# Max-pool and subtract: the first tile loaded in pieces of 1, 1 and 2 rows

## The chip, the cores and the metric

One core of one Trainium2 chip runs the program. The metric is the device time of one execution in microseconds (us). The profile's span is 1.7 to 1.8 us shorter than that time, because it begins with the first and ends with the last recorded instruction. VectorE is called DVE in the profile, the queue that issues loads SP, the queue that issues stores ACT. "Packet" means one of the transfers that a DMA engine makes; the trace records each one with its start, its duration and its size.

## The reference

```
x: (8, 64, 256, 256) float32
pooled    = max over each 8 x 8 window of x
upsampled = pooled, each value repeated over its 8 x 8 window
out       = x - upsampled
```

The kernel calls 8 image rows of one channel a "row": 2048 floats, 8 KB, in one partition. A tile of 4 rows on 128 partitions is 4.19 MB, and there are 32 tiles. Everything is read once and written once: 134.22 MB in and 134.22 MB out.

## The kernel before

A ring of six tile slots in SBUF. SP issues the loads and waits before each reuse of a slot for its stores; DVE reduces and subtracts in place; ACT issues the stores. TensorE only passes on "loaded" semaphores. The parts that matter, with cuts marked:

```python
HEAD = [2, 2]; SIZE = 4; ROUNDS = 5; TAIL = [2, 1, 1]; SLOTS = 6
...
for i in range(len(sizes)):                      # SP
    slot = slot_of(i)
    if landed[slot]:
        nc.sync.wait_ge(stored[slot], 16 * landed[slot])
    for k, (lo, R) in enumerate(cuts(HEAD if i == 0 else [sizes[i]])):
        ... nc.sync.dma_start(out=sbuf(i, lo, R), in_=dram(x_rows, i)[:, part]).then_inc(...)
...
for lo, R in cuts(HEAD):                         # DVE
    take(filled, 1)
    pool_and_subtract(sbuf(0, lo, R), top(0, lo, R), R)
with nc.vector.Fori(0, ROUNDS):
    with nc.vector.Fori(0, SLOTS) as slot:
        take(filled, 1)
        pool_and_subtract(ring[...slot...], tops[...slot...], SIZE)
```

`pool_and_subtract` is one `tensor_reduce` over the piece and one `tensor_tensor` per row.

## Time and profile before

| | before |
|---|---|
| time, median of the 3 first runs | 627.96 us (627.55 to 628.2) |
| span of the profiled run | 625.5 us |
| DVE busy | 562.6 us, 90% |
| DMA rate, 117 to 577 us | 433 GB/s |
| DVE starts / first store is issued | 8.47 / 17.57 us |
| DVE starts the last tile | 597.89 us |

The busy lines, the windows and the head of the timeline are shown in the prediction. One more part of the page of the kernel before is needed later, the DMA issues; its columns are tensors, queue, operation and count, KB each, and the median time from issue to landing in us.

```profile
ring<-in_x_dram SPq DMA_DIRECT2D x31, 4096.0 KB, 62.1
out_dram<-ring ACTq DMA_DIRECT2D x30, 4096.0 KB, 35.9
```

Two transfers of 4.19 MB take 19.4 us at 433 GB/s. A load takes 62 us and a store 36 us, so most of that is time in a queue: more than three loads and nearly two stores are always under way.

### The profile page before, as it was taken

The numbers are of one execution on the slowest core, as the hardware profiler recorded it, in microseconds if no ns is written. First come the engines' busy times: TensorE is split into PE (matmuls) and PEld (weight loads), VectorE is DVE, ScalarE is ACT, GpSimd is POOL, SyncE is SP. The second block draws the span as 40 slices with busy tenths as digits, with TensorE's granted clock in tenths as the row PEclk, the third lists the DMA queues.
The fourth block names the chain that finished last, engine by engine and source line by source line (L and its number), as shares of the span: only waits on it lengthen the run. The fifth ranks groups of instructions, "written<-read, shape, count | busy, mean of one in ns | idle before, by whom it ended". The sixth has DMA issues, their size and how long they took to land. (4 is left out here: it accounts for less than half of the span.)

```text
span 625.5 us, 613 instructions
## 1 busy us (share of the span) xinstructions
DVE 562.6 (90%) x163; POOL 0.2 (0%) x4
## 2 busy tenths in 40 slices
DVE  4999999998898888988889888898888998888983
POOL 0000000000000000000000000000000000000000
DMA  8999999999999999999999999999999999999998
GB/s 369 402 434 438 436 434 436 434 436 434 434 432 427 425 434 436 436 436 434 436 434 436 434 434 427 430 425 436 436 436 434 436 436 434 434 436 434 425 427 363
DMA packets 9792, 268.44 MB, mean 429 GB/s; under 512 B 1088, under 2 KB 1088, under 8 KB 1088
## 3 DMA queue, kind: packets, MB, share of 16 engines
q1 hardware_dynamic: 4752, 134.22, 49.9%
q10 hardware_dynamic: 5040, 134.22, 49.7%
HBM read 134.22 MB, written 134.22 MB: 429 GB/s over the span
## 5 line engine op out<-in xcount | busy, mean ns | idle before, releaser
L81 DVE TENSOR_REDUCE tops<-ring (+2 forms) x35 | 278.4, 7953 | 48.4 <-DVEq L75 48.4
L93 DVE TENSOR_TENSOR ring<-ring,tops (+1 forms) x128 | 285.0, 2287 | 5.2 <-DVEq L75 0.2
L164 POOL MEMSET const-bfloat16-1.0<- 128x1 bf16 x1 | 0.1, 102 | 0.0
L164 POOL MEMSET const-uint8-127<- 128x1 uint8 x1 | 0.1, 102 | 0.0
L164 POOL MEMSET const-float32-0.0<- 128x1 f32 x1 | 0.1, 99 | 0.2 <-issue 0.2
L164 POOL MEMSET const-float32-1.0<- 128x1 f32 x1 | 0.1, 99 | 0.0
## 6 DMA issues: line engine op xcount, KB each, us to landing
ring<-in_x_dram SPq DMA_DIRECT2D x31, 4096.0 KB, 62.1
out_dram<-ring ACTq DMA_DIRECT2D x30, 4096.0 KB, 35.9
out_dram<-ring ACTq DMA_DIRECT2D x3, 2048.0 KB, 19.3
ring<-in_x_dram SPq DMA_DIRECT2D x2, 2048.0 KB, 9.5
out_dram<-ring ACTq DMA_DIRECT2D x2, 1024.0 KB, 9.2
```

The lines of the kernel that those rows point to most:

```text
L81: nc.vector.tensor_reduce(out=maxs if R > 1 else maxs[:, 0], in_=(wins.rearrange("p r ph ow pw -> p r ow ph pw") if R > 1 else wins[:, 0]. ...
L93: sub = nc.vector.tensor_tensor(out=wins[:, r], in0=wins[:, r], in1=maxs[:, r].unsqueeze(1).unsqueeze(3).to_broadcast([P, pH, oW, pW]), op ...
L164: nc = _bacc.Bacc("TRN2", target_bir_lowering=False, num_devices=1)
```

## The change

The intent is to let DVE begin on one row instead of two and to send the first store sooner. The first tile is loaded as 1, 1 and 2 rows; it is stored as 2 and 2 rows as before. DVE waits directly on the load's semaphore for the first and the last tile, the wait for the maximum in these two tiles is a plain wait in place of `take`, which also counts the semaphore down, and the two nested loops become one whose slot is a remainder. The core of the diff, with cuts marked:

```diff
-HEAD = [2, 2]
-SIZE = 4
-ROUNDS = 5
+HEAD, HEAD_OUT = [1, 1, 2], [2, 2]
+SIZE, TILES = 4, 30
...
-        for lo, R in cuts(HEAD):
+        for k, (lo, R) in enumerate(cuts(HEAD)):
+            nc.vector.wait_ge(first[k], 16)
+            pool_and_subtract(sbuf(0, lo, R), top(0, lo, R), R, k + 1)
+        with nc.vector.Fori(0, TILES) as i:
+            slot = i % SLOTS
             take(filled, 1)
-            pool_and_subtract(sbuf(0, lo, R), top(0, lo, R), R)
-        with nc.vector.Fori(0, ROUNDS):
-            with nc.vector.Fori(0, SLOTS) as slot:
...
```

More of the change, by code (lines that the diff above doesn't have):

```diff
@@ L33 @@
     out_rows = out.rearrange("b c (oh ph) w -> (b c oh) (ph w)", ph=pH)
-    sizes = [sum(HEAD)] + [SIZE] * (ROUNDS * SLOTS) + [sum(TAIL)]
+    sizes = [sum(HEAD)] + [SIZE] * TILES + [sum(TAIL)]
     assert sum(sizes) * P == x_rows.shape[0] and max(sizes) == SIZE
@@ L47 @@
     reduced = tc.alloc_semaphore("reduced")
+    pooled = tc.alloc_semaphore("pooled")
     ready = tc.alloc_semaphore("ready")
@@ L75, in take, with pool_and_subtract @@
         nc.vector.wait_ge(sem, n).then_inc(sem, -n)
-    def pool_and_subtract(part, top, R):
+    def pool_and_subtract(part, top, R, nth=None):
         wins = part.rearrange("p (r ph ow pw) -> p r ph ow pw", r=R, ph=pH, ow=oW)
@@ L89, in pool_and_subtract @@
             op=mybir.AluOpType.max,
-        ).then_inc(reduced, 1)
-        take(reduced, 1)
+        ).then_inc(reduced if nth is None else pooled, 1)
+        if nth is None:
+            take(reduced, 1)
+        else:
+            nc.vector.wait_ge(pooled, nth)
         for r in range(R):
@@ L112 @@
                 )
-                landed[slot] += 1
-        for k in range(len(HEAD)):
-            nc.tensor.wait_ge(first[k], 16).then_inc(filled, 1)
-        for i in range(1, len(sizes)):
+            landed[slot] += len(HEAD_OUT) if i == 0 else 1
+        for i in range(1, last):
             turn = (i - 1) // SLOTS + 1
@@ L124 @@
         for i in range(len(sizes)):
-            for lo, R in cuts(HEAD if i == 0 else TAIL if i == last else [SIZE]):
+            for lo, R in cuts(HEAD_OUT if i == 0 else TAIL if i == last else [SIZE]):
                 part = slice(lo * ROW, (lo + R) * ROW)
-                done += 1
+                done = [sum(HEAD[: k + 1]) for k in range(len(HEAD))].index(lo + R) + 1 if i == 0 else done + 1
                 nc.scalar.wait_ge(ready, done)
@@ L133 @@
         nc.scalar.wait_ge(final, 16 * n_final)
-        for lo, R in cuts(HEAD):
-            take(filled, 1)
-            pool_and_subtract(sbuf(0, lo, R), top(0, lo, R), R)
-        with nc.vector.Fori(0, ROUNDS):
-            with nc.vector.Fori(0, SLOTS) as slot:
-                take(filled, 1)
-                pool_and_subtract(
-                    ring[:, bass.ds(slot * (SIZE * ROW), SIZE * ROW)],
-                    tops[:, bass.ds(slot * (SIZE * oW), SIZE * oW)],
-                    SIZE,
-                )
-        take(filled, 1)
-        for lo, R in cuts(TAIL):
-            pool_and_subtract(sbuf(last, lo, R), top(last, lo, R), R)
+        for k, (lo, R) in enumerate(cuts(HEAD)):
[3 more added lines that the diff above has]
+            slot = i % SLOTS
+            take(filled, 1)
+            pool_and_subtract(
+                ring[:, bass.ds(slot * (SIZE * ROW), SIZE * ROW)],
+                tops[:, bass.ds(slot * (SIZE * oW), SIZE * oW)],
+                SIZE,
+            )
+        nc.vector.wait_ge(loaded[slot_of(last)], 16 * ((last - 1) // SLOTS + 1))
+        for k, (lo, R) in enumerate(cuts(TAIL)):
+            pool_and_subtract(sbuf(last, lo, R), top(last, lo, R), R, len(HEAD) + k + 1)
 _INS = ['x']
```

## The prediction

> **What bounds the kernel now.** I read the page first, then the windows, the timeline of the first 70 us and the waits, and last single landings (the tile view of `ring` over a window that holds one issue).
>
> The page gives the two candidates, VectorE and the transfers:
>
> ```profile
> span 625.5 us, 613 instructions
> ...
> DVE 562.6 (90%) x163; POOL 0.2 (0%) x4
> ...
> DMA  8999999999999999999999999999999999999998
> GB/s 369 402 434 438 436 434 436 434 436 434 434 432 427 425 434 436 436 436 434 436 434 436 434 434 427 430 425 436 436 436 434 436 436 434 434 436 434 425 427 363
> ```
>
> VectorE (DVE) is busy 90% of the span, the DMA row is at its top digit in all slices but the first and the last, and the rate is flat. 268.44 MB have to move (134.22 in, 134.22 out, from the page's queue part). The chain of waits on the page is of no use here: it holds only the last subtraction, because the chain does not follow transfers. So I ask the windows whether the rate depends on the stage:
>
> ```profile
> core 0: us, DVE busy (x) POOL busy (x), PEclk, DMA share, GB/s
> 4.00:17.50 13.50, 8.88 (x4) 0.00 (x0) 1.00 1.04 448
> 17.50:26.50 9.00, 8.85 (x5) 0.00 (x0) 1.00 0.98 384
> 26.50:36.50 10.00, 9.84 (x3) 0.00 (x0) 1.00 1.02 441
> 36.50:117.00 80.50, 79.91 (x25) 0.00 (x0) 1.00 1.00 431
> 117.00:577.00 460.00, 419.63 (x120) 0.00 (x0) 1.00 1.00 433
> ```
>
> The last column is what to see: about 430 GB/s while there are only loads (4 to 17.5 us; the short windows err at their edges, since one round of 32 KB packets on 16 engines is 0.5 MB), 431 and 433 with loads and stores mixed, and 419 in a further window, 598 to 622 us, that has stores alone. The DMA share is 1.00 throughout. DVE on the other hand has 40 us of idle time in the 460 us window. Its waits between 132 and 600 us sum to 40.0 us in 25 waits, the longest 1.6, all for a load (the semaphore that `take` reads). The SP queue in turn waits 522.6 us for landed stores (26 waits). So it is a closed ring of six tiles in which the DMA engines are the slow station: one tile in and one out, 8.39 MB, at 433 GB/s is 19.4 us per tile, against 17.65 us of DVE work per tile (44.07 to 61.72 in the timeline below the head). **The transfers set the period, not DVE.**
>
> The head, in the timeline:
>
> ```profile
> 8.47 4.42 DVE L81 TENSOR_REDUCE tops<-ring 128x64 f32<-128x4096 f32 x1 [8.47 <-DVEq L75]
> 13.04 4.49 DVE L93 TENSOR_TENSOR ring<-ring,tops 128x2048 f32<-128x2048 f32 x2
> 17.45 4.41 DVE L81 TENSOR_REDUCE tops<-ring 128x64 f32<-128x4096 f32 x1
> 17.57 44.60 ACTq L129 DMA_DIRECT2D out_dram<-ring  x4
> 22.01 4.49 DVE L93 TENSOR_TENSOR ring<-ring,tops 128x2048 f32<-128x2048 f32 x2
> 26.42 8.68 DVE L81 TENSOR_REDUCE tops<-ring  x1
> ```
>
> DVE sits idle 8.47 us for the first two rows, and the first store goes out at 17.57. But the SP queue issues seven loads back to back from 0.94 to about 4 us (landing views: issues at 0.9, 1.4, 1.8, 2.3, 2.9 and on), 24 rows or 25.2 MB, 58 us of work at 433 GB/s. The engines have all they can carry from about 2 us on, with or without stores.
>
> At the end: the last load is issued at 535.5 and lands 62.1 us later, at 597.6; DVE starts the last tile at 597.89 and the last store is issued at 616.2 and lands 8.1 us later. The three last stores (1, 1 and the 2 rows before them) land at 606.98 + 12.5 = 619.5, 611.6 + 10.3 = 621.9 and 616.25 + 8.1 = 624.4: steps of 2.4 us for 1 MB, that is the DMA rate again. They queue behind each other, so the end is set by the bytes as well.
>
> **What the Trainium skill says.** "DMA: Bandwidth & Descriptors", section "Where 436 GB/s comes from", puts the ceiling of the 16 engines at 435 GB/s; the trace agrees, with 433 in the long window. The same page, "Issuing engines are not separate DMA queues", says loads from one engine and stores from another end on the same 16 engines and interleave; here too, the two queues have 50.2% and 50.1% between 120 and 570 us. Its section "Queues, rings and completion order" says that an engine alternates between queues packet by packet. The trace agrees: between 24 and 36 us the 2-row stores (16 KB runs) move 1.61 MB while the 4-row loads (32 KB runs) move 3.67. "VectorE: DVE Perf Modes", "The perf-mode tier table", has an fp32 tensor_tensor of 2048 elements at 2293 ns and tensor_reduce without a faster mode; the trace has 2285 to 2291, and 2278 for a reduce of 2048. So DVE work is proportional to rows, and cutting a piece in two costs only a small fixed part.
>
> **The change part by part.**
>
> 1. First load of 2 rows becomes two of 1 row. The first 2 MB landed 7.3 us after issue, the second 2 MB at 1.36 + 11.8 = 13.1, 4.9 us after the first: 2.45 us per MB and so a fixed part of 7.3 − 4.9 = 2.4. A 1 MB load should land 2.4 + 2.45 = 4.9 us after its issue, at 5.8 instead of 8.2. DVE starts at about 6.0 (8.47 before): 2.5 us earlier.
> 2. DVE work of the head: the pieces of one row take 4.63 us each start to start (tail: 606.87 to 611.50), two of them 9.26 against 8.98 for a piece of two (8.47 to 17.45): 0.28 more. First store at 6.0 + 9.26 = 15.3, 2.3 us earlier. The third piece, 8.97 us, ends at 24.2 instead of 26.42.
> 3. What waits there: tile 1. Its load (issued at 1.8, 23.4 us to landing) came at 25.2 before. DVE would now stand ready 1.0 us before that. And the earlier store takes its share from this very load: 2.3 us at 31% of the rate is 2.3 × 0.31 = 0.7 us of delay, landing at about 25.9. So tile 1 starts near 26.1, where it was 26.42. Of 2.2 us won, about 0.3 is left, and a new idle of nearly 2 us stands before tile 1.
> 4. From tile 1 to tile 7 DVE runs without a wait at 17.65 us per tile (before 133.33 us no wait of any size). It keeps the 0.3 us. From tile 7 on the loads decide, and the loads come as the bytes allow.
> 5. Bytes: none removed, none added (one more load of 16 semaphore writes). An earlier store means load-only time replaced by mixed time, at the same 430 to 433 GB/s. Worth at most 2.3 us × 1% = 0.02 us.
> 6. The PE relay for the first and last tile goes: about 0.1 us of semaphore hops before DVE, at the head (already counted) and the tail, where DVE's output waits in the store queue anyway (8.1 us to landing where 1 MB needs 4.9).
> 7. The flat loop with the slot as a remainder: a few register instructions per tile in place of the inner loop's. DVE's queue runs ahead of its engine during the four subtractions (8.9 us), and where some lands behind the wait it lies in 1.5 us of slack per tile. Worth 0.
>
> Sum: 0.0 to −0.3 us at the end of the span.
>
> **The rivals.**
>
> *Carry-through:* the 2.3 us of the first store arrive at the end, 627.96 − 2.3 = 625.7. For it: the first store is what releases the second turn of its slot. Against it: that release, at 51 us, is for a load that queues behind three others, and the DMA row has no hole in which the time could be won. Even this is 0.37%, within 2%.
>
> *DVE becomes the bound:* if the remainder costs more than the 1.5 us slack per tile, and is not hidden, each further microsecond costs 30 us. At 2.5 us it would be 658. Against it: the nested loop's own register work shows no gap between a tile's last subtraction and the next reduce before 133 us (44.07 + 8.68 to 52.90 is only the wait on the maximum).
>
> *The transfers get worse:* 8 KB runs instead of 16 KB for 2 MB, or an unlucky alternation of queues. The 1-row stores at the end land 2.4 us apart, at the full rate, so small runs cost nothing visible. The dip in 17.5 to 26.5 us (384 GB/s, up to 0.8 us together with the window after it) sits at the first store; if it is tied to that store it moves with it, and may change by some tenths.
>
> **Range and chances.** Bytes at 433 GB/s are 620 us of the 625.5, and none of them moves. Take 0.2 off: 627.8. Executions spread 627.55 to 628.2; with another session and the dip, 626.6 to 628.9 should hold it 8 times in 10. Faster than 2% would need 12.6 us, which no step here has; slower by 2% needs the second rival. Faster 0.01, same 0.98, slower 0.01.
>
> **What would show it.** In the changed profile: first reduce near 6.0; first store near 15.3; a new idle of 1.5 to 2.2 us before tile 1 near 26.1; waits of about 1.5 us per tile from tile 7 on; 433 GB/s in the middle; last load landing within 0.5 us of 597.6. It would be wrong if the rate in the middle differs, if DVE's waits vanish and its per-tile time goes over 19.4 us, or if the last load lands 2 us earlier.

## The result, and the profile after

| | before | after |
|---|---|---|
| time, median of 6 runs each | 627.48 us (627.32 to 628.2) | 627.52 us (627.2 to 628.55) |
| ratio | | 1.0, 95% interval 0.9987 to 1.0013 |
| DVE starts | 8.47 us | 5.84 us |
| first store is issued | 17.57 us | 15.01 us |
| DVE starts tile 1 | 26.42 us | 26.29 us |
| DVE starts the last tile | 597.89 us | 600.13 us |

A ratio here is the mean time of one kernel's fast runs over that of the other's fast runs of the same rounds, so it is not quite the ratio of the medians.

The head of the timeline of the changed kernel; the columns are start, duration, engine, line, operation, tensors, shapes and count, and in brackets the idle time before and what ended it:

```profile
5.84 2.29 DVE L81 TENSOR_REDUCE tops<-ring 128x32 f32<-128x2048 f32 x1 [5.84 <-DMA ring<-in_x_dram]
...
14.89 4.41 DVE L81 TENSOR_REDUCE tops<-ring 128x64 f32<-128x4096 f32 x1
15.01 9.20 ACTq L130 DMA_DIRECT2D out_dram<-ring  x2
19.34 4.49 DVE L96 TENSOR_TENSOR ring<-ring,tops 128x2048 f32<-128x2048 f32 x2
26.29 8.69 DVE L81 TENSOR_REDUCE tops<-ring  x1 [2.46 <-DVEq L75]
```

The change does what it was made for: DVE starts 2.6 us and the first store leaves 2.6 us sooner. The last line shows where the time goes: an idle of 2.46 us that was not there before stands in front of tile 1, and DVE starts that tile only 0.13 us earlier than it did.

The windows of the changed kernel, over the stretches that the prediction shows of the kernel before; the last two columns are the DMA share and rate:

```profile
4.00:17.50 13.50, 11.59 (x5) 0.00 (x0) 1.00 1.07 447
17.50:26.50 9.00, 6.50 (x4) 0.00 (x0) 1.00 0.93 370
26.50:36.50 10.00, 9.85 (x2) 0.00 (x0) 1.00 1.03 446
36.50:117.00 80.50, 78.62 (x25) 0.00 (x0) 1.00 1.00 433
117.00:577.00 460.00, 418.38 (x119) 0.00 (x0) 1.00 1.00 433
```

DVE does more in the first window (11.59 us against 8.88) and less in the second (6.50 against 8.85). The rate of the DMA engines is the same in every stretch to within the edges of the windows. And the DMA issues of the changed kernel:

```profile
ring<-in_x_dram SPq DMA_DIRECT2D x31, 4096.0 KB, 65.5
out_dram<-ring ACTq DMA_DIRECT2D x30, 4096.0 KB, 32.4
```

A store now lands 3.5 us sooner after its issue and a load 3.4 us later. The head has moved the queues against each other and left their sum alone (98.0 us before, 97.9 after, from the medians).

The profiled run of the changed kernel was the slowest of its six: span 626.8 us, the other five 625.4 to 625.8. Two windows at its end show why:

```profile
619.00:623.40 4.40, 0.00 (x0) 0.00 (x0) 1.00 1.00 423
623.40:625.00 1.60, 0.00 (x0) 0.00 (x0) 1.00 0.06 26
```

At 623.4 us the rate falls from 423 to 26 GB/s, one sixteenth: a single one of the 16 DMA engines works 1.6 us longer than the rest. Such a straggler is worth remembering for the experiments. The other five runs were not profiled; their spans leave room for less of it or none. Whether the change has a part in it is not shown.

### The profile page after: what moved, and what is told of

Read it like the earlier page. It is cut to its first block, busy times and chain, and to the rows that moved or that the text cites. A ratio compares the mean times of both kernels' runs of the same rounds, so it can differ in the third digit from the quotient of the medians.

```text
span 626.8 us, 619 instructions
## 1 busy us (share of the span) xinstructions
DVE 562.9 (90%) x164; POOL 0.2 (0%) x4
## 5 line engine op out<-in xcount | busy, mean ns | idle before, releaser
L81 DVE TENSOR_REDUCE tops<-ring (+2 forms) x36 | 278.5, 7735 | 50.4 <-DVEq L75 43.3
## 6 DMA issues: line engine op xcount, KB each, us to landing
ring<-in_x_dram SPq DMA_DIRECT2D x31, 4096.0 KB, 65.5
out_dram<-ring ACTq DMA_DIRECT2D x3, 2048.0 KB, 19.6
```

What stands on the lines that cost most here:

```text
L81: nc.vector.tensor_reduce(out=maxs if R > 1 else maxs[:, 0], in_=(wins.rearrange("p r ph ow pw -> p r ow ph pw") if R > 1 else wins[:, 0]. ...
```

## The experiments

The theory: the DMA engines carry all they can from 2 us on, so the end is set by the bytes, and what the head wins is waited away. The rivals: two effects of 2.3 us that cancel (the head wins what the new loop loses); DVE as the true bound; a head that counts in the end. Each edit is against the changed kernel.

**Do two effects cancel?** First the new head with the old nested loop, then the new loop with the old head.

```diff
-        with nc.vector.Fori(0, TILES) as i:
-            slot = i % SLOTS
+        with nc.vector.Fori(0, TILES // SLOTS):
+            with nc.vector.Fori(0, SLOTS) as slot:
```

> The new head and the direct waits, with the old nested loop. Theory (the bytes set the end): 627.5 us, within 0.2% of before. Rival (the head wins its 2.3 us and the flat loop loses as much, so that the two cancel): 625.2 us here, 0.37% faster.

```diff
-HEAD, HEAD_OUT = [1, 1, 2], [2, 2]
+HEAD, HEAD_OUT = [2, 2], [2, 2]
```

> The flat loop and the direct waits with the old head of 2 and 2 rows. Theory: 627.5 us, within 0.2% of before; tile 1 starts near 26.4 us with no long wait in front. Rival (the flat loop costs what the head wins): 629.8 us.

The head alone took 627.45 us (ratio 1.0, interval 0.9983 to 1.0017), the loop alone 628.05 us (1.0009, 0.9992 to 1.0026). Neither has an effect of the 2.3 us (0.37%) that the rival needs, so no two such effects cancel. DVE starts tile 1 after an idle of 2.81 us with the new head alone (first line) and without a wait with the old one (second line):

```profile
26.53 8.69 DVE L81 TENSOR_REDUCE tops<-ring  x1 [2.81 <-DVEq L75]
```

```profile
26.11 8.68 DVE L81 TENSOR_REDUCE tops<-ring  x1
```

**Is the early store what holds up tile 1?** The first tile loaded in three pieces but stored in one.

```diff
-HEAD, HEAD_OUT = [1, 1, 2], [2, 2]
+HEAD, HEAD_OUT = [1, 1, 2], [4]
```

> The first tile still loaded as 1, 1 and 2 rows but stored in one piece of 4, so the first store goes out near 23.9 instead of 15.0 us. Theory (the early store took its share from the load of tile 1): that load lands near 25.2 us as before instead of 25.8, VectorE starts tile 1 about 0.6 us earlier than in the changed kernel, near 25.7, the last load lands earlier than 600.1, near 592 to 596, and the time is 627.5 us, within 0.2%. Rival (the first store's time counts at the end): slower by up to the 8.9 us that it is later, 636 us.

627.46 us (0.9998, 0.9982 to 1.0015): the first store leaves 8.6 us later than in the changed kernel and the time stays. The timeline of this kernel from its third piece on:

```profile
19.10 4.50 DVE L96 TENSOR_TENSOR ring<-ring,tops 128x2048 f32<-128x2048 f32 x2
23.52 8.68 DVE L81 TENSOR_REDUCE tops<-ring  x1
23.63 0.38 ACTq L130 DMA_DIRECT2D out_dram<-ring  x1
```

Tile 1 follows at 23.52 us with no idle time in front. With no store beside it the load had landed, at 22.7 us, before DVE was free. So it is the early store that held up the load of tile 1. My number for the landing (25.2 us) was too late, because in the kernel before, too, a store at 17.57 us had slowed this load. DVE is now 2.8 us ahead of the changed kernel at tiles 1 to 3, and that is worth nothing either: the lead is waited away at tiles 4 to 6, and DVE starts tile 6 at 115.85 us (115.88). The second expectation was wrong: I expected the last load to land sooner, at 592 to 596 us, and it lands at 600.29, no sooner than in the changed kernel (600.10). The packet records suggest why. The two-row stores move in packets of 16 KB and took 31% of the engines' time in the kernel before (24 to 36 us); this store of four rows moves in packets of 32 KB, like the loads, and takes 52% (30 to 44 us). So the load of tile 3 lands at 57.26 us, where it landed at 57.33. No run changes the packet size alone.

**What if the head is made much worse?** The first tile in one piece; and a start that waits for tile 4.

```diff
-HEAD, HEAD_OUT = [1, 1, 2], [2, 2]
+HEAD, HEAD_OUT = [4], [4]
```

> The first tile loaded and stored in one piece of 4 rows, so VectorE starts near 13.3 us and the first store goes out near 31 us. Theory (the loads that are queued from the start fill the engines until about 60 us): 627.5 us, within 0.3% of before. Rival (the time to the first store counts): 627.5 + 16 = 643 us; half of it if it counts in part.

```diff
+        nc.vector.wait_ge(loaded[slot_of(4)], 16)
         for k, (lo, R) in enumerate(cuts(HEAD)):
             nc.vector.wait_ge(first[k], 16)
```

> The changed kernel with one more wait before VectorE's first piece: for the load of tile 4, which lands when 20 rows have come, near 50.5 us. Theory (only a DMA queue that runs empty costs time): the 24 queued rows are through at about 60 us, the first store comes at about 59.8 and the second at 68.7, so the engines stand idle some 10 us in the stretch from 60 to 100 us, and the time is 636 to 643 us. Rival A (the head never matters): 627.5. Rival B (all of the later start counts): 627.5 + 44.7 = 672 us.

The late start took 641.79 us, one run, inside the range of the theory and far from both rivals (627.5 and 672). Its DMA row and rates, in 40 slices of 16 us:

```profile
DMA  8999698899999999999999999999999999999998
GB/s 369 442 434 390 265 426 326 330 434 446 430 426 426 442 442 426 426 432 449 430 426 426 440 444 426 426 430 449 432 426 426 440 442 428 426 430 446 432 428 360
```

The holes are in slices 4 to 8, 48 to 128 us. The last queued load lands at 61.7 us, and the next one is issued only at 76.3, when the first tile has been stored and its slot is free. With 46 us of delay in DVE's start (51.98 us instead of 5.84) the end moves by some 14 us. The window from 57 to 117 us, of the changed kernel and then of this one, with the DMA share and rate in the last two columns:

```profile
57.00:117.00 60.00, 58.28 (x19) 0.00 (x0) 1.00 1.00 433
57.00:117.00 60.00, 59.48 (x18) 0.00 (x0) 1.00 0.86 353
```

353 GB/s in place of 433 is 60 x (1 - 353 / 433) = 11 us alone, and with a DMA share of 0.86 most of it is time in which the engines had too little to do.

The kernel with one piece took 630.95, 631.79 and 631.38 us, and 640.56 in a fourth run; the ratio, 1.0113 (1.0038 to 1.0187), has that run in it (the other three alone: 1.006). That is 4 us more than expected and 12 less than the rival has. The windows at its end:

```profile
619.00:623.40 4.40, 0.00 (x0) 0.00 (x0) 1.00 0.93 395
623.40:625.00 1.60, 0.00 (x0) 0.00 (x0) 1.00 0.07 31
625.00:627.80 2.80, 0.00 (x0) 0.00 (x0) 1.00 0.06 23
```

From 623.4 us on 31 and then 23 GB/s are left, and 433 / 16 is 27: one of the 16 DMA engines is still at work, and the packet records show the other 15 done by 623.6. So these 4 us are one engine that falls behind. In the records of this profile 35 packets after 40 us are 0.03 to 0.35 us longer than others of their size, 4.0 us together; the profiles of the kernel before and of the changed kernel have none. The sum fits the lag, but the trace does not say which engine moved a packet, nor why these took longer. To see whether the late first store brings it about, two more kernels hold DVE until the whole first tile has landed, with the tile loaded in three pieces or in two.

```diff
-HEAD, HEAD_OUT = [1, 1, 2], [2, 2]
+HEAD, HEAD_OUT = [1, 1, 2], [4]        # the second kernel: [2, 2], [4]
...
+        nc.vector.wait_ge(first[2], 16)   # the second kernel: first[1]
         for k, (lo, R) in enumerate(cuts(HEAD)):
```

> The first tile loaded as 1, 1 and 2 rows, but VectorE is held until all four rows have landed (13.2 us), and the tile is stored in one piece, so the first store goes out near 31.4 us, as it did in the kernel that loads the tile in one piece and took 631.6 us. Theory (the late first store is hidden; those 4 us come from one of the 16 DMA engines that ends 4 us after the other 15, an accident of that kernel's load pieces): 627.5 us, within 0.3%, the other 15 engines again done at 623.4 us. Rival (the late first store itself costs it): 631.6 us.

> The same hold with the first tile loaded as 2 and 2 rows. Theory: 627.5 us, within 0.3%. Rival (the late first store itself costs it): 631.6 us. If one of the two held kernels shows it and the other not, what decides is how the 16 engines fall in against each other, and neither theory nor rival covers it.

With three pieces it took 627.3 us (0.9996, 0.9979 to 1.0012), the first store at 31.07 us, 16 us later than in the changed kernel. So a late first store by itself costs nothing. With two pieces four runs took 631.63 to 632.19 us and the profiled one 627.72 (median 632.02; the ratio, 1.0069, 1.0052 to 1.0086, leaves the profiled run out); the first store of the profiled run left at 31.08 us. These 4 us thus come with a late first store behind larger load pieces, and not in every execution. The slow-engine picture stands in one profile, that of the one-piece kernel; the runs of 632 us were not profiled. What makes one engine fall behind stays open.

Two lines of the timeline at the end, the first of the kernel held with three pieces, the second of the changed kernel:

```profile
592.82 4.42 DVE L81 TENSOR_REDUCE tops<-ring 128x64 f32<-128x4096 f32 x1 [1.19 <-DMA ring<-in_x_dram]
```

```profile
600.13 4.42 DVE L81 TENSOR_REDUCE tops<-ring 128x64 f32<-128x4096 f32 x1 [1.24 <-DMA ring<-in_x_dram]
```

The kernel whose DVE begins 7 us later has its last load 7 us earlier, and both take 627.3 to 627.5 us. So the split between the queues moves and the end does not. When the stores begin is one part of this split: beside an earlier store the loads fall back. It is not the only one, as the kernel with one store has shown: its first store leaves 8.6 us later than in the changed kernel, and its last load lands no sooner.

**Do the bytes set the end?** Tiles 15 and 16 store half their rows (a wrong result).

```diff
+                if i in (15, 16):
+                    R = R // 2
                 part = slice(lo * ROW, (lo + R) * ROW)
```

> Wrong result on purpose: tiles 15 and 16 store only two of their four rows, 4.19 MB less in the middle of the run, with every instruction of VectorE kept. Theory (bytes at 433 GB/s set the end): 9.7 us less, 617.8 us. Rival (VectorE's chain or the head and tail set the end): no change, 627.5 us.

617.59 us (0.9849, 0.9833 to 0.9865), 9.7 us less than the 627.24 us of before in the same rounds, as the bytes have it: 4.19 MB / 433 GB/s = 9.7 us. It makes no difference that they are taken from the middle.

**How much can DVE lose before it counts?** One more reduce per tile, of 1024 and of 4096 elements.

```diff
             take(filled, 1)
+            nc.vector.tensor_reduce(out=junk[:, : 1024 // 8],   # the second kernel: 4096
+                in_=ring[:, bass.ds(slot * (SIZE * ROW), 1024)].rearrange("p (a b) -> p a b", b=8),
+                axis=mybir.AxisListType.X, op=mybir.AluOpType.max)
```

> One more reduce of 1024 elements per tile on VectorE, an estimated 1.2 us from 2.28 us for 2048, so 18.9 us per tile against 19.4 us of transfers. Theory: 627.5 us, within 0.3%; the waits before the reduces shrink from about 1.3 to some tenths. Rival (VectorE sets the period): 30 x 1.2 = 36 us more, 663 us.

> One more reduce of 4096 elements per tile, 4.4 us, so VectorE needs 22.07 us per tile and becomes the slow station. Theory: 26.3 + 30 x 22.07 + 18.2 + about 5 for the last store + 3 outside = 715 us. Rival (VectorE has set the end all along): 627.5 + 30 x 4.42 = 760 us.

The first took 627.76 us (1.0006, 0.999 to 1.0023), the second 710.33 us in one run. The busy line of the first kernel's page, its line of the waits (engine, line, what was waited for; us, times, longest), and then the busy line of the second:

```profile
DVE 595.8 (95%) x194; POOL 0.2 (0%) x4
```

```profile
DVE junk L144 <- DVEq L76: 10.8, 16, 2.7
```

```profile
DVE 690.4 (97%) x194; POOL 0.2 (0%) x4
```

33 us more of DVE work came out of its waits, which shrank from 43.3 us (26 waits) to 10.8 (16 waits). The larger addition, 128 us of work (690.4 less 562.9), made DVE the bound: 83 us slower than before, not 128 or 132, since the 40 us of waits of the kernel before were free here too, and since the span now ends 5.0 us after DVE and not 9.3, the last store having nothing queued before it: 127.5 - 40 - 4.3 = 83. My estimate of 715 was 5 us too high because a tile took 21.97 us and not 22.07, and 1.8 us and not 3 lay outside the span.

**What is the dip at the first store?** Both kernels move less for some microseconds there. The windows of the changed kernel:

```profile
4.00:17.00 13.00, 11.09 (x5) 0.00 (x0) 1.00 1.02 434
17.00:24.00 7.00, 6.80 (x3) 0.00 (x0) 1.00 1.02 382
24.00:37.00 13.00, 10.55 (x2) 0.00 (x0) 1.00 1.00 430
```

I tried to spend the dip ahead of time, with a transfer of 64 KB on the ACT queue at the very start: a store of zeros to rows that are overwritten later (issued at 1.2 us; its packets move from 4.7 to 5.7 us, so beside the loads), and a load (issued at 0.9 us).

```diff
+        nc.gpsimd.memset(warm[:], 0.0).then_inc(pooled_warm, 1)
+        nc.scalar.wait_ge(pooled_warm, 1)
+        nc.scalar.dma_start(out=dram(out_rows, last)[:, :128], in_=warm[:]).then_inc(warmed, 16)
+        # the second kernel instead: nc.scalar.dma_start(out=warm[:], in_=dram(x_rows, last)[:, :128])...
```

> The changed kernel with a store of 64 KB on the ACT queue at the very start (zeros into rows that the last tile overwrites later, after a wait). It asks what the dip near the first store is: in both kernels the load packets that run as the first store starts take 1.6 to 1.9 us instead of 1.21. Theory A (it belongs to the first DMA of the ACT queue) and theory B (it belongs to the first write to HBM): the dip near 17 to 20 us is gone and the time is 0.5 to 0.8 us less, 626.8. Theory C (it comes whenever stores begin beside a stream of loads): the dip stays, 627.5 us.

> The changed kernel with a load of 64 KB on the ACT queue at the very start. Theory A (first DMA of the ACT queue): the dip near 17 to 20 us is gone, 0.5 to 0.8 us less, 626.8. Theory B (first write to HBM) and theory C (stores beginning beside loads): the dip stays, 627.5 us.

627.75 us and 627.87 us (each 1.0004, 0.9991 to 1.0018), and the dip is still there, 412 and 410 GB/s in the same 7 us; a window this short can't tell whether it is smaller than the 382. In the packet records the 32 KB packets take 1.21 us. In the kernel before, 22 of the 3,968 load packets of that size take more than 1.4 us, all of them between 19.6 and 22.1 us; in the changed kernel all 44 lie between 16.1 and 23.4 us. In the kernel with the store at 23.63 us all but one lie at 25.5 to 27.5, in the held one with the store at 31.07 us at 32.8 to 34.8. (The expectation has 1.6 to 1.9 us for such packets; the records have 1.4 to 2.3 us before and 1.4 to 1.7 in the changed kernel.) So the dip goes with the first large store beside a stream of loads, from 1 to 3 us after its issue on, and neither the first transfer of a queue nor the first write is its cause; the small store beside loads did not bring it. Added up and divided by 16 engines, what these packets take too long is an estimated 0.6 to 1.0 us, once in every version but the late start. There 85 packets between 77 and 127 us are slow, 3.4 us in the same sum.

No version with a right result beats the kernel before.

## Why the prediction was right

Its time held (627.52 us for 627.8 predicted, and the difference to before is none). Step by step:

- Steps 1 and 2, the start: reduce at 5.84 us (about 6.0 predicted), first store at 15.01 us (15.3). A one-row piece took 4.53 us from start to start, not 4.63, because with the plain wait the subtraction starts 0.03 us after the reduce (0.15 with `take`).
- Step 3, tile 1: its load landed at 2.3 + 23.5 = 25.8 us (25.9 predicted), DVE started it at 26.29 (26.1) after an idle of 2.46 us (nearly 2). The kernel with one store shows the reason: without the early store the idle is gone.
- Step 4, the stretch to tile 7: nearly right. The first wait came at tile 6 already, 1.26 us before 115.88 us, since the load of that tile landed at 115.4 us, where it had landed at 113.6 before, and DVE was free at 114.6. So the small lead was not kept to tile 7: DVE starts tile 6 later than before, 115.88 us against 114.64.
- Step 5, the bytes: 433 GB/s in the long window before and after, and 9.7 us less when 4.19 MB are left out.
- Steps 6 and 7, relay and loop: 628.05 us for both with the old head, not told apart from before.
- The rivals: DVE as bound is refuted by the added reduce (33 us of work for no time), the carry-through by the kernel held with three pieces (16 us of delay for no time); the 4 us of the kernels with larger pieces are a quarter of that delay, and their cause is open. That the transfers get worse is not seen: 433 GB/s in both.
- One reading is a little narrow: the subtractions of the kernel before take 2281 to 2294 ns, not 2285 to 2291.

One sentence of it was wrong: that the last load would land "within 0.5 us of 597.6". It landed 65.5 us after its issue at 534.6, so at 600.1 us. I had taken "the loads come as the bytes allow" for each queue alone. The bytes fix only the sum of both. An earlier store takes its share from the loads, and the loads carry this lag to the end: 0.6 us at tile 1, 1.8 at tile 3, 2.5 at the last. There was room for it: the two last stores of 1 MB still took 8.5 us (median) from issue to landing, where the first load of 1 MB took 4.9. Step 6 had named this room; that a lag of the last load would have to fit into it was not foreseen.

## What to carry to other kernels

Before shortening a start, look at how long a load takes from issue to landing: if it is several times its own bytes over the rate, as here, the queue is full from the start and the first piece's latency is hidden, up to the point where that queue runs empty (46 us of delay cost 14). A gain ahead of saturated DMA engines is given back at the next load that they deliver; follow it to the first wait after the change. What still counted here was bytes, and time in which a queue ran empty.

## What the Trainium skill lacked or had wrong

- "DMA: Bandwidth & Descriptors", section "Where 436 GB/s comes from": it says that for transfers between HBM and SBUF the HBM side at about 358 GB/s binds. One core alone, reading and writing, moved 433 GB/s for 460 us here, at the fabric figure of the same section. The page's own table has 425 for loads of one core with the pair's other core idle, and the page gives about 358 to each where both stream; the sentence needs this condition.
- The same page, "Queues, rings and completion order", tells how an engine alternates between queues, but not what happens as a second queue joins a busy one: 32 KB packets of 1.21 us that started 2.1 to 4.5 us after the issue of the first store took up to 2.3 us (kernel before), an estimated 0.7 us lost, and a small transfer ahead of time did not prevent it.
- The same page, "Latency and other measured facts", has a first byte after about 600 ns for HWDGE. Counted from the end of the issuing instruction the first load packet agrees, 0.6 us (0.94 + 0.37 to 1.93 us, kernel before). The first store packet beside running loads moved 3.3 us after that end (17.57 + 0.38 to 21.22); the page has no figure for such a full queue.
- No page gives a size for how far one engine falls behind in a kernel like this: one of 16 ended 1.6 us after the others in the profile of the changed kernel and 4.2 us after them in that of the one-piece kernel.
